# Two fused blocks on one core: where b_down's weighted sum is made, where the context's split parts are kept, and in what order the middle section stands against the context's products

## The chip, the cores and the metric

The kernel runs on one core of a Trainium2 chip. The metric is the device time of one execution in microseconds (us); the time before the change is 2914.66 us, the median of 3 runs. TensorE (PE) has two clock levels, 1.2 and 2.4 GHz; the profile gives the granted clock of a stretch as a share of the higher level, so 0.50 is 1.2 GHz.

## The reference

Two blocks run one after the other on 512 tokens of width 1024, all in float32. Cut to what the change touches:

```
# block 1: a mixer (left out), then a mixture of 32 experts, top 4
hn2 = rmsnorm(h) * (1 + sc2) + sh2
top_val, top_idx = top_k(hn2 @ router_w + router_b, 4);  gate = softmax(top_val)
for each expert e, on its own tokens x:
    g, up = split(x @ w_gu[e] + b_gu[e])
    act = (clip(up, -7, 7) + 1) * (min(g, 7) * sigmoid(1.702 * min(g, 7)))
    y[e] = act @ w_down[e] + b_down[e]
ff = sum over a token's four experts of gate * y[e]
x  = h + g2 * rmsnorm(ff)
# block 2: attention over a window, a state space model, attention over all, a gated FFN
xc  = rms_norm(ctx) * a + s                 # 256 context tokens
xn  = rms_norm(x) * a' + s'                 # 512 latent tokens (the output of block 1)
kv, dt, xbc of the context = xc @ columns of w_in
... of the latents         = xn @ columns of w_in, and so on to the output
```

b_down enters the sum as `sum_e G[token, e] * b_down[e]`, one product of the 512x32 gate matrix G with the 32x1024 matrix of biases.

## The kernel before

**Products.** TensorE multiplies in a reduced float32 form, so each operand is split into a high and a low part (`hi`, `lo`; `turnh`, `turnl`; `chh`, `chl`) and a product is made of three: hi x hi, hi x lo, lo x hi. All large weights come through one `Stream`: chunks of 128x1024 (512 KB) are loaded on the SyncE queue (SP) into `raw` tiles, ScalarE casts each to `hi` (L1573), VectorE subtracts to `lo` (L1575). Pools of three raw and three hi/lo buffers each are filled ahead of use, in the order of a list of requests; the last entry of a request says which pools it may take.

**Experts.** The router gives G. Then `go_on` runs 32 expert blocks of 128 tokens. Within them PE, ScalarE, VectorE and GpSimd (POOL) keep the order in which the code is written. Each block has three products (gate, up, down, of 8 weight chunks each), and a dictionary of hooks names what else is called behind chunk number 0 to 7 of a product: activations, transposes of the next operand, the gather of the next tokens, the scatter of the finished rows `ey` to `y_d` (L1286). Before the loop `start_sums` (L1104) transposes G to `gT`, multiplies it with `bdown` and copies the result to `k.acc`, the tile in which the four rows of each token are added later.

**Context.** `fr.b2.context()` is a generator that normalises the 256 context tokens. It is stepped once per expert from the third on, by the hook behind chunk 6 of the gate product. Each of its last steps handles one or two of 8 column groups: transposes on PE, scale and shift on VectorE (`ctmp`, L1782), the high part on ScalarE (`chp`, L1843), the low part on POOL (`clp`), and, each second group, two stores to DRAM (`chh_d`, `chl_d`) on ScalarE's queue:

```
nc.scalar.copy(part[0][:, j % 2], o)
nc.gpsimd.tensor_tensor(part[1][:, j % 2], o, f(part[0][:, j % 2]), op=OP.subtract)
if j % 2:
    for v, d in zip(part, s.ch_d):
        nc.scalar.dma_start(d[:, j - 1:j + 1], f(v))
```

**Behind the experts.** `mid` (L2767) makes block 1's result. For each of 4 tiles of 128 tokens it loads four 128x1024 tiles of rows, `my`, from `y_d` on POOL's queue (three buffers), adds each with its gate on VectorE (L2790, `scalar_tensor_tensor`), takes the norm (ScalarE squares, POOL's power `mr`, VectorE L2795 and L2796), stores x to `x_d` on ScalarE's queue, and takes the second norm (`mq`), whose factor VectorE multiplies in (L2800). `go_on` drains `mid` before `Block2.run` (L2570) starts. `run` loads `chh` and `chl` back from DRAM on SP, takes eight steps of `J.ctx` (the context's products with w_in, L1726, and L135 to L137 with the operands turned round; `put_kv` rotates and stores the keys, L1982 to L1998), then weaves the context's state space steps and the transposes of the latents (`turned_g`) with the rest of `J.ctx`, and goes on to the latents' products. From `mid` on the framework's scheduler sets each engine's order, by what is ready in the order of the code.

Of the kernel before, what the change touches and what calls it, by code (L numbers as in the profile page):

```python
# [10 lines left out]
F32 = mybir.dt.float32  # L11
# [1013 lines left out]
def router(k, A, pool, lg, counted):  # L1025
# [70 lines left out]
    k.gk = k.mk.tile([P, NT, TOPK], F32, name="gk")  # L1096
# [6 lines left out]
def start_sums(k, A, pool, G):  # L1103

    nc = k.nc
    E = NE
    bd = pool.tile([E, D], F32, name="bdown")
    nc.scalar.dma_start(bd, A["exp_b_down"][0])
    gT = pool.tile([E, T], F32, name="gT")
# [12 lines left out]
class Experts:  # L1122
# [156 lines left out]
    def out(s, b, step=None):  # L1279
        nc = s.nc  # L1280
        if step in (0, None):
            b.y = s.pool.tile([P, D], F32, name="ey", tag="ey", bufs=2)
# [76 lines left out]
def experts(fr, k, A, lg, mod1):  # L1359
# [29 lines left out]
    k.acc = k.hp.tile([P, NT, D], F32, name="acc", tag="h")  # L1389
# [38 lines left out]
    def go_on():  # L1428
# [3 lines left out]
        start_sums(k, A, rt, G)  # L1432
# [16 lines left out]
        with tc.manual_schedule(engines={E.PE, E.Activation, E.DVE, E.Pool}):  # L1449
# [3 lines left out]
            for e in range(NE):  # L1453
# [5 lines left out]

                def act(half):  # L1460
                    return lambda: x.acted(b, half)
# [3 lines left out]
                x.gate(nb, {0: act(0), 1: act(1), 3: turn(0), 4: turn(1), 6: lambda: next(side, None) if e > 1 else None})  # L1465
# [13 lines left out]
                if e + 2 == NE:  # L1479
# [6 lines left out]
                    mid = fr.b2.mid()  # L1486
                    next(mid)
# [4 lines left out]
        drain(mid)  # L1492
# [303 lines left out]
class Block2:  # L1796
# [18 lines left out]
    def context(s):  # L1815
# [11 lines left out]
        s.ch_d = [k.dp.tile([P, KJ, 256], F32, name=n) for n in ("chh_d", "chl_d")]  # L1827
# [10 lines left out]
        part = []  # L1838

        def put(j, o):  # L1840
            if j % 2 == 0:
                part[:] = [p.tile([P, 2, 256], F32R, name=n, tag=n, bufs=2) for n in ("chp", "clp")]
            nc.scalar.copy(part[0][:, j % 2], o)  # L1843
            nc.gpsimd.tensor_tensor(part[1][:, j % 2], o, f(part[0][:, j % 2]), op=OP.subtract)
            if j % 2:
# [724 lines left out]
    def run(s):  # L2570
# [23 lines left out]
        for _ in range(8):  # L2594
            next(J.ctx)
# [293 lines left out]
```

## Time and profile before

| | |
|---|---|
| median of 3 runs | 2914.66 us (2907.94 to 2918.86) |
| the profiled execution | 2916.79 us, its span 2915.0 us |
| mean granted clock | 0.962 |
| PE busy | 2697.6 us, 93% of the span |
| VectorE busy | 2197.3 us, 75% |
| ScalarE busy | 1595.3 us, 55% |
| experts, first product to last | about 420 to 1653 us from the span's start |

Times of the trace count from the start of the span. "Busy" of an engine includes matmuls that run slowly under the lower clock. In the rows of a timeline, a bracket gives how long the engine stood idle before the instruction and what released it.

### The profile page before, as it was taken

Reading aid. Unit: us, or ns where it says so; the run is one execution under the profiler, and the core shown is the slowest. Engines: PE = TensorE matmul, PEld = TensorE weight load, DVE = VectorE, ACT = ScalarE, POOL = GpSimd, SP = SyncE. Lnnn points to the kernel's source line nnn. Section 1 sums busy time; section 2 is a strip of 40 time slices with the busy share of each in tenths; the row PEclk is TensorE's granted clock in tenths of the full one; section 3 lists DMA queues with packets and bytes.
Section 4 is the critical chain, followed back from the end, with each engine's and each line's share of the span. In section 5 each row is a group of like instructions: output and inputs, shape, how many; then the busy total and the mean of one; then the engine's idle time right before and its main releaser. Section 6 shows DMA issues by size and latency. Waiting matters only on the chain. (4 is left out here: it accounts for less than half of the span.)

```text
span 2915.0 us, 37354 instructions
## 1 busy us (share of the span) xinstructions
PE 2697.6 (93%) x12897; PEld 2140.3 (73%) x12897; DVE 2197.3 (75%) x3214; ACT 1595.3 (55%) x2403; POOL 597.2 (20%) x460
## 2 busy tenths in 40 slices
PE   6789889999999999999999849998999999899998
PEld 3566638887777778888878647887688787688886
DVE  6988559999999999999999777766777555533322
ACT  3233337787777677777777543664457422443322
POOL 2654110102000010110000022001421332322222
PEclk8889889999999999999999979999999999999999
DMA  7546558999999999999999942221211565433332
GB/s 209 171 125 196 188 213 299 378 355 358 353 336 360 337 371 355 373 358 376 368 356 366 346 148 91 62 66 44 65 30 48 189 200 173 142 94 94 95 94 72
DMA packets 273119, 645.33 MB, mean 221 GB/s; under 512 B 53754, under 2 KB 99744, under 8 KB 272414
## 3 DMA queue, kind: packets, MB, share of 16 engines
q1 hardware_dynamic: 227728, 587.41, 57.5%
q10 hardware_dynamic: 33390, 30.30, 3.3%
q0 software_dynamic: 11808, 25.19, 2.4%
q8 instruction: 103, 1.69, 0.2%
q14 instruction: 90, 0.74, 0.1%
HBM read 624.33 MB, written 34.73 MB: 226 GB/s over the span
## 5 line engine op out<-in xcount | busy, mean ns | idle before, releaser
L1575 DVE TENSOR_TENSOR lo<-raw,hi 128x1024 fp32r<-128x1024 f32 x938 | 1115.5, 1232 | 303.6 <-ACT hi L1573 301.8
L1573 ACT CAST hi<-raw 128x1024 fp32r<-128x1024 f32 x997 | 1011.2, 1056 | 458.9 <-PE mm L136 132.2
L1232 PE MATMUL mm<-hi,turnh 128*128 128x512 f32 x1584 | 506.1, 401 | 0.8 <-ACT hi L1573 0.8
L1232 PE MATMUL mm<-lo,turnh 128*128 128x512 f32 x1584 | 495.2, 394 | 11.2 <-DVE lo L1575 10.8
L1232 PE MATMUL mm<-hi,turnl 128*128 128x512 f32 x1584 | 495.8, 394 | 0.0
L1232 PEld LDWEIGHTS mm<-lo,turnh 128*128 128x128 f32 x1584 | 295.9, 188 | 88.9 <-DVE lo L1575 22.7
L1232 PEld LDWEIGHTS mm<-hi,turnl 128*128 128x128 f32 x1584 | 298.4, 188 | 68.4 <-issue 1.5
L1232 PEld LDWEIGHTS mm<-hi,turnh 128*128 128x128 f32 x1584 | 287.8, 189 | 56.0 <-ACT hi L1573 2.5
L1575 POOL TENSOR_TENSOR lo<-raw,hi 128x1024 fp32r<-128x1024 f32 (+1 forms) x59 | 148.9, 2524 | 558.7 <-ACT hi L1573 524.0
L1286 POOL DMA_INDIRECT y_d<-ey,idx x33 | 50.4, 1527 | 877.7 <-ACT ey L1284 723.9
L141 ACT CAST turnh<-tr 128x512 fp32r<-128x512 f32 x132 | 77.5, 587 | 188.0 <-PE tr L221 188.0
L135 PE MATMUL mm<-lhh,hi 128*128 128x512 f32 x288 | 118.9, 413 | 0.7 <-ACT apr L2068 0.7
L1661 DVE SCALAR_TENSOR_TENSOR mvacc<-mvw,silu_c,mvacc 128x512 f32<-128x512 f32 x112 | 101.7, 908 | 22.4 <-DMA mvw<-in_w_mod_dram 17.1
L137 PE MATMUL mm<-lhh,lo 128*128 128x512 f32 x288 | 117.3, 409 | 0.0
L136 PE MATMUL mm<-lhl,hi 128*128 128x512 f32 x288 | 115.5, 401 | 0.0
L142 DVE TENSOR_TENSOR turnl<-tr,turnh 128x512 fp32r<-128x512 f32 x132 | 90.4, 685 | 4.5 <-ACT turnh L141 4.3
L2053 DVE TENSOR_REDUCE amax<-mm 128x1 f32<-128x256 f32 (+2 forms) x128 | 60.4, 501 | 41.1 <-PE mm L2048 21.1
L1726 PE MATMUL mm<-hi,lhh 128*128 128x256 f32 (+2 forms) x256 | 85.5, 338 | 3.2 <-DVE zt L2384 1.9
L2068 ACT ACTIVATE apr<-mm,negm 128x256 f32<-128x256 f32 (+2 forms) x128 | 68.6, 543 | 30.8 <-DVE negm L2058 16.4
L1726 PE MATMUL mm<-lo,lhh 128*128 128x256 f32 (+2 forms) x256 | 83.3, 326 | 1.9 <-DVE lo L1575 1.9
L1726 PE MATMUL mm<-hi,lhl 128*128 128x256 f32 (+2 forms) x256 | 82.2, 324 | 0.0
L137 PE MATMUL mm<-fhh,lo 128*128 128x512 f32 x192 | 77.2, 402 | 0.0
(752 smaller groups left out, 5168.9 us busy)
## 6 DMA issues: line engine op xcount, KB each, us to landing
raw<-in_exp_w_gu_dram SPq DMA_DIRECT2D x528, 512.0 KB
raw<-in_exp_w_down_dram SPq DMA_DIRECT2D x264, 512.0 KB
raw<-in_w_in_dram SPq DMA_DIRECT2D x83, 512.0 KB
mvw<-in_ada_w_dram SPq DMA_DIRECT2D x32, 512.0 KB
raw<-in_w_out_dram SPq DMA_DIRECT2D x32, 512.0 KB
mvw<-in_w_mod_dram SPq DMA_DIRECT2D x32, 512.0 KB
raw<-in_ffn_w_gate_dram SPq DMA_DIRECT2D x22, 512.0 KB
raw<-in_ffn_w_up_dram SPq DMA_DIRECT2D x22, 512.0 KB
```

Source lines behind the costliest of these rows:

```text
L135: k.nc.tensor.matmul(out, lh, rh, start=start, stop=False)
L136: k.nc.tensor.matmul(out, lh, rl, start=False, stop=False)
L137: k.nc.tensor.matmul(out, ll, rh, start=False, stop=stop)
L141: k.nc.scalar.copy(hi, src)
L142: k.nc.vector.tensor_tensor(lo, src, f(hi), op=OP.subtract)
L1232: nc.tensor.matmul(pss[n], a[:, j, :], c[:, n * 512:(n + 1) * 512], start=(j == 0 and i == 0), stop=(last and i == 2))
L1573: s.k.nc.scalar.copy(pm(hi[:, :m], True), pm(raw[:, :m], False))
L1575: eng.tensor_tensor(pm(lo[:, :m], True), pm(raw[:, :m], False), pm(f(hi[:, :m]), True), op=OP.subtract)
L1661: nc.vector.scalar_tensor_tensor(acc, v[:, j - q], sc(j), acc, op0=OP.mult, op1=OP.add)
L1726: k.nc.tensor.matmul(o, a[:, jj, sl], c[:, j, :], start=(jj == 0 and u == 0 and i % per == 0), stop=(jj == nk_all - 1 and u == 2), skip_gr ...
L2053: nc.vector.tensor_reduce(mx[:, i_:i_ + 1], ps[:, :n], axis=AX.X, op=OP.max)
L2068: nc.scalar.activation(b.pr[:, o:o + n // P].rearrange("p a n -> p (a n)"), ps[:, :n], AF.Exp, bias=b.nm, scale=0.125, accum_out=tile_[t]. ...
```

## The change

1. `start_sums` becomes `gates_turned`: only the transposes of G, and a store of `gT` to DRAM. The product with `bdown` is made in `mid`, per token tile, into PSUM, and the first `my` of a tile is added to it from there, in two halves.
2. The context's parts stay on chip, in a tile `chb` (in the space that `k.acc` had). Its steps are finer: transposes, then VectorE, then ScalarE, then POOL, each in a step of its own, and three hooks per expert call them (`aside`: gate 6, down 4, up 3).
3. `mid` is called in `run` and woven with `J.ctx`. All its DMAs are on POOL's queue, `my` has five buffers, its result stands in a tile `xn`, and the last factor is multiplied in by ScalarE.
4. The context's weight chunks take pool 0 alone. `ey` has one buffer, `k.gk` lies in the space of `lg`.

```diff
-def start_sums(k, A, pool, G):
+def gates_turned(k, pool, G):
...
     for t in range(NT):
-        nc.tensor.transpose(pt[:E, t * P:(t + 1) * P], G[:, t, :], k.ident)
-    nc.scalar.copy(gT, pt[:E, :])
-    for t in range(NT):
-        for n in range(2):
-            ps = tr_ps(k)
-            nc.tensor.matmul(ps, gT[:, t * P:(t + 1) * P], bd[:, n * 512:(n + 1) * 512], start=True, stop=True)
-            nc.scalar.copy(k.acc[:, t, n * 512:(n + 1) * 512], ps)
+        nc.tensor.transpose(pt[:NE, t * P:(t + 1) * P], G[:, t, :], k.ident)
+    nc.scalar.copy(gT, pt[:NE, :])
+    nc.gpsimd.dma_start(k.gT_d, gT)
...
-                x.gate(nb, {0: act(0), 1: act(1), 3: turn(0), 4: turn(1), 6: lambda: next(side, None) if e > 1 else None})
+                x.gate(nb, {0: act(0), 1: act(1), 3: turn(0), 4: turn(1), 6: aside})
...
-                hooks = {0: first, 1: lambda: x.gated(nb, 1), 2: lambda: x.gated(nb, 2), 5: step}
+                hooks = {0: first, 1: lambda: x.gated(nb, 1), 2: lambda: x.gated(nb, 2), 4: aside, 5: step}
                 x.down(b, hooks)
-                hooks = {0: lambda: x.out(b, 0), 1: lambda: x.out(b, 1), 2: step, 7: step}
+                hooks = {0: lambda: x.out(b, 0), 1: lambda: x.out(b, 1), 2: step, 3: aside, 7: step}
...
-        drain(mid)
...
+        s.chb = k.hp.tile([P, 2, KJ, 256], F32R, name="chb", tag="h")
...
-        yield from turned_g(k, tmp, xc, 2, s.a1[:, 1], s.s1[:, 1], put, 0)
+        for j in range(KJ):
+            ps = sm_ps(k)
+            for t in range(2):
+                nc.tensor.transpose(ps[:, t * P:(t + 1) * P], xc[:, t, j * P:(j + 1) * P], k.ident)
+            yield
+            o = p.tile([P, 256], F32, name="ctmp", tag="ctmp", bufs=2)
+            nc.vector.tensor_scalar(o, ps[:, :256], s.a1[:, 1, j:j + 1], s.s1[:, 1, j:j + 1], op0=OP.mult, op1=OP.add)
+            yield
+            nc.scalar.copy(s.chb[:, 0, j], o)
+            yield
+            nc.gpsimd.tensor_tensor(s.chb[:, 1, j], o, f(s.chb[:, 0, j]), op=OP.subtract)
...
-            k.st.reqs[i][5][:] = [both] * 2
+            k.st.reqs[i][5][:] = [(0,)] * 2
...
-        for v, d in zip((S.chh, S.chl), s.ch_d):
-            nc.sync.dma_start(f(v), d)
+        s.xn = chp.tile([P, NT, D], F32, name="xn")
+        middle = s.mid()
...
-        for _ in range(8):
-            next(J.ctx)
+        weave(middle, J.ctx, rate=0.6)
...
     def mid(s):
...
+        nc.gpsimd.dma_start(gT, k.gT_d)
...
-        nc.scalar.dma_start(g2b, k.g2_d.partition_broadcast(P))
+        nc.gpsimd.dma_start(bd, s.A["exp_b_down"][0])
+        nc.gpsimd.dma_start(g2b, k.g2_d.partition_broadcast(P))
...
-            nc.scalar.dma_start(hs[t], k.h_d[t * P:(t + 1) * P, :])
+            nc.gpsimd.dma_start(hs[t], k.h_d[t * P:(t + 1) * P, :])
...
-                y = p.tile([P, D], F32, name="my", tag="my", bufs=3)
+                y = p.tile([P, D], F32, name="my", tag="my", bufs=5)
                 nc.gpsimd.dma_start(y, rows[:, i])
-                nc.vector.scalar_tensor_tensor(x, y, k.gk[:, t, i:i + 1], x, op0=OP.mult, op1=OP.add)
+                if i:
+                    nc.vector.scalar_tensor_tensor(x, y, k.gk[:, t, i:i + 1], x, op0=OP.mult, op1=OP.add)
+                    continue
+                for n in range(2):
+                    c = slice(n * 512, (n + 1) * 512)
+                    ps = sm_ps(k)
+                    nc.tensor.matmul(ps, gT[:, t * P:(t + 1) * P], bd[:, c], start=True, stop=True)
+                    nc.vector.scalar_tensor_tensor(x[:, c], y[:, c], k.gk[:, t, i:i + 1], ps, op0=OP.mult, op1=OP.add)
+            yield 5.0
...
-            nc.scalar.dma_start(k.x_d[t * P:(t + 1) * P, :], h)
+            nc.gpsimd.dma_start(k.x_d[t * P:(t + 1) * P, :], h)
...
-            nc.vector.tensor_scalar(x, h, q[:, o], None, op0=OP.mult)
+            nc.scalar.mul(x, h, q[:, o])
...
+            yield 4.0
```

Three places where the order of instructions changes. The first is PE at the start of the experts, behind the products `TW,oh` that make the first slots; `mm<-hi,turnl` and its like are expert 0's gate product. Before:

```order
L1169 MATMUL sm<-TW,oh 128x4
L1232 MATMUL mm<-hi,turnl 128x512
L1117 MATMUL tr<-bdown,gT 128x512 x8
L1232 MATMUL mm<-hi,turnl 128x512
L1232 MATMUL mm<-lo,turnh 128x512 x2
L1232 MATMUL mm<-hi,turnh 128x512 x2
```

After the change, at the same place:

```order
L1162 MATMUL sm<-TW,oh 128x4
L1225 MATMUL mm<-hi,turnl 128x512 x2
L1225 MATMUL mm<-lo,turnh 128x512 x2
L1225 MATMUL mm<-hi,turnh 128x512 x2
L1225 MATMUL mm<-hi,turnl 128x512 x2
```

The eight products with `bdown` no longer stand between the two halves of the gate product's first chunk.

The second place is ScalarE within one of the experts that take a context step; `turnh` are the next operand's parts, `esg` the gate's sigmoid, `ey` the finished rows. Before, between the casts of weights:

```order
L141 CAST turnh<-tr 128x512
L1573 CAST hi<-raw 128x1024 x2
L1843 CAST chp<-ctmp 128x256
L1847 DMA chh_d<-chp 128x512
L1847 DMA chl_d<-clp 128x512
L1573 CAST hi<-raw 128x1024 x2
L1252 ACTIVATE esg<-mm 128x512 x2
```

After the change:

```order
L1245 ACTIVATE esg<-mm 128x512 x2
L1566 CAST hi<-raw 128x1024 x8
L1277 COPY ey<-mm 128x512 x2
L1566 CAST hi<-raw 128x1024 x3
L1840 CAST chb<-ctmp 128x256
L1566 CAST hi<-raw 128x1024
L141 CAST turnh<-tr 128x512
```

The cast of the context's part now stands one hook behind the VectorE instruction that writes `ctmp`, and the two stores, which wait for POOL's `clp`, are gone from ScalarE's queue.

The third place is VectorE behind the last expert; `kk` and `ks` are the context's keys, `my` the rows of block 1. Before, the context's keys stand behind all of `mid`, the end of which is:

```order
L2796 TENSOR_TENSOR mh<-mh,acc 128x1024
L149 TENSOR_SCALAR mq<-mq 128x1
L2800 TENSOR_SCALAR acc<-mh,mq 128x1024
L1982 COPY kk<-mm 128x128
L1989 TENSOR_TENSOR kk<-kk,khi 128x128
L1990 COPY ks_16013<-khi 128x2x128
```

After the change, right behind the last expert:

```order
L1568 TENSOR_TENSOR lo<-raw,hi 128x1024
L1975 COPY kk<-mm 128x128
L1568 TENSOR_TENSOR lo<-raw,hi 128x1024
L2788 SCALAR_TENSOR_TENSOR xn<-my,lg,sm 128x512 x2
L1982 TENSOR_TENSOR kk<-kk,khi 128x128
L2782 SCALAR_TENSOR_TENSOR xn<-my,lg,xn 128x1024
L1983 COPY ks_15881<-khi 128x2x128
L1984 COPY ks_15881<-kk 128x2x128
L2782 SCALAR_TENSOR_TENSOR xn<-my,lg,xn 128x1024
```

The first context keys stand among the first token tile's sums (`sm` is b_down's product, `lg` holds the gates). On POOL's queue (after the change) the loads of `gTb`, `bdown`, `g2b` and two `mh` stand ahead of the last scatter, and the later `mh` loads and the `x_d` stores between the `my` loads:

```order
L1279 DMA y_d<-ey,idx 2048x1024
L2780 DMA my<-y_d 128x1024 x7
L152 TENSOR_TENSOR mr<-mr,mhalf 128x1
L2780 DMA my<-y_d 128x1024 x2
L2796 DMA x_d<-mh 128x1024
L2780 DMA my<-y_d 128x1024
L152 TENSOR_TENSOR mq<-mq,mhalf 128x1
```

There a `my` load now stands behind a store that waits for VectorE's `mh`; before, the stores were on ScalarE's queue.

## Rows read from the trace of the kernel before

**Rows 1.** The page: busy time and slices; DMA is the engines' mean share.

```profile
PE 2697.6 (93%) x12897; PEld 2140.3 (73%) x12897; DVE 2197.3 (75%) x3214; ACT 1595.3 (55%) x2403; POOL 597.2 (20%) x460
...
PE   6789889999999999999999849998999999899998
...
PEclk8889889999999999999999979999999999999999
```

**Rows 2.** Windows: stretch, length, busy PE, PEld, DVE, ACT, POOL, PEclk, DMA, GB/s.

```profile
419.00:437.00 18.00, 17.48 (x36) 6.74 (x36) 6.32 (x13) 8.85 (x13) 1.98 (x2) 0.50 0.63 226
437.00:500.00 63.00, 63.00 (x292) 51.33 (x293) 55.94 (x60) 48.21 (x55) 3.94 (x2) 0.96 0.83 286
760.00:1050.00 290.00, 277.74 (x1269) 216.98 (x1268) 267.69 (x297) 207.72 (x248) 21.39 (x23) 1.00 0.95 349
1050.00:1600.00 550.00, 547.95 (x2563) 447.46 (x2562) 541.55 (x604) 425.64 (x488) 55.56 (x31) 1.00 0.98 365
1653.40:1720.00 66.60, 19.77 (x108) 18.80 (x108) 40.58 (x46) 15.67 (x26) 17.31 (x25) 0.63 0.81 265
1720.00:1790.00 70.00, 60.12 (x401) 53.15 (x402) 55.28 (x106) 34.18 (x68) 21.64 (x15) 0.94 0.17 56
```

**Rows 3.** Timeline of PE at the start of the experts: start, duration, instruction.

```profile
421.89 0.77 PE L1232 MATMUL mm<-hi,turnl 128*128 128x512 f32 x1
422.89 14.02 PE L1117 MATMUL tr<-bdown,gT 32*128 32x512 f32 x16 [0.23 <-ACT gT L1113]
436.84 0.80 PE L1232 MATMUL mm<-hi,turnl 128*128 128x512 f32 x1
```

**Rows 4.** Timeline of DVE in the same stretch and in the first expert.

```profile
438.75 1.23 DVE L1575 TENSOR_TENSOR lo<-raw,hi 128x1024 fp32r<-128x1024 f32 x1 [12.85 <-ACT hi L1573]
...
454.08 0.69 DVE L1257 SCALAR_TENSOR_TENSOR eg<-mm,esg 128x512 f32<-128x512 f32 x1
```

**Rows 5.** Timeline around one of the context's steps within the experts.

```profile
805.13 0.41 ACT L1843 CAST chp<-ctmp 128x256 fp32r<-128x256 f32 x1 [4.07 <-DVE ctmp L1782]
...
806.83 2.00 ACT L1573 CAST hi<-raw 128x1024 fp32r<-128x1024 f32 x2 [1.29 <-POOL clp L1844]
...
807.90 1.22 DVE L1575 TENSOR_TENSOR lo<-raw,hi 128x1024 fp32r<-128x1024 f32 x1 [2.81 <-ACT hi L1573]
```

**Rows 6.** Waits from 480 to 1640 us: total, times, longest.

```profile
ACT chp L1843 <- DVE ctmp L1782: 30.5, 8, 4.1
...
PE mm L1232 <- DVE lo L1575: 10.8, 18, 1.9
```

**Rows 7.** Timeline behind the experts, 1653 to 1721 us.

```profile
1653.75 1.06 ACT L1284 COPY ey<-mm 128x512 f32<-128x512 f32 x2
...
1662.56 0.58 PE L1726 MATMUL mm<-hi,chh 128*128 128x288 f32 x1 [9.34 <-DMA chh<-chh_d]
...
1670.20 3.95 DVE L2790 SCALAR_TENSOR_TENSOR acc<-my,gk,acc 128x1024 f32<-128x1024 f32 x3 [15.10 <-DMA my<-y_d]
...
1718.34 0.75 DVE L2800 TENSOR_SCALAR acc<-mh,mq 128x1024 f32<-128x1024 f32 x1 [0.66 <-POOL mq L152]
...
1720.34 1.08 PE L1994 MATMUL tr<-ident,ks 128*128 128x128 f32 x4 [32.48 <-DVE ks L1990]
```

**Rows 8.** VectorE's first instruction for the latents' state space steps.

```profile
1789.29 0.48 DVE L2244 MEMSET acsrw<- 64x512 f32 x1
```

**Rows 9.** The tile `my`: duration in ns min/median/max, first and last start.

```profile
L2789 POOL DMA_DIRECT2D my<-y_d x16: 527/532/582, 1664.4 to 1701.1; - x16
L2790 DVE SCALAR_TENSOR_TENSOR acc<-my,gk,acc x16: 1275/1280/1286, 1670.2 to 1709.0; 128x1024 f32<-128x1024 f32 x16
...
DMA to landing us min/median/max: 4.4/5.8/7.3
```

**Rows 10.** The tile `mh`: VectorE's multiplication by the last factor.

```profile
L2800 DVE TENSOR_SCALAR acc<-mh,mq x4: 748/753/754, 1693.5 to 1718.3; 128x1024 f32<-128x1024 f32 x4
```

**Rows 11.** DMA issues from 1620 to 1800 us: the scatters, median us to landing.

```profile
y_d<-ey,idx POOLq DMA_INDIRECT x2, 8.6
```

More of the change, by code (lines that the diff above doesn't have):

```diff
@@ L1094, in router @@
     TT(G, G, gs.unsqueeze(2).to_broadcast(sh), OP.mult)
-    k.gk = k.mk.tile([P, NT, TOPK], F32, name="gk")
+    k.gk = lg[:, :, :TOPK]
     for i in range(TOPK):
@@ L1100, in router @@
     return G
-def start_sums(k, A, pool, G):
+def gates_turned(k, pool, G):
     nc = k.nc
[L1106 to L1109, printed above, removed]
+    gT = pool.tile([NE, T], F32, name="gT")
     pt = tr_ps(k)
     for t in range(NT):
-        nc.tensor.transpose(pt[:E, t * P:(t + 1) * P], G[:, t, :], k.ident)
-    nc.scalar.copy(gT, pt[:E, :])
-    for t in range(NT):
-        for n in range(2):
-            ps = tr_ps(k)
-            nc.tensor.matmul(ps, gT[:, t * P:(t + 1) * P], bd[:, n * 512:(n + 1) * 512], start=True, stop=True)
-            nc.scalar.copy(k.acc[:, t, n * 512:(n + 1) * 512], ps)
+        nc.tensor.transpose(pt[:NE, t * P:(t + 1) * P], G[:, t, :], k.ident)
+    nc.scalar.copy(gT, pt[:NE, :])
+    nc.gpsimd.dma_start(k.gT_d, gT)
 class Experts:
@@ L1281, in out @@
         if step in (0, None):
-            b.y = s.pool.tile([P, D], F32, name="ey", tag="ey", bufs=2)
+            b.y = s.pool.tile([P, D], F32, name="ey", tag="ey", bufs=1)
             for n in range(2):
@@ L1431, in go_on @@
         nb = x.block(1)
-        start_sums(k, A, rt, G)
+        gates_turned(k, rt, G)
         es1.close()
@@ L1458, in go_on, with aside @@
                     queue.append(x.further(0, fu))
+                def aside():
+                    if e > 1:
+                        next(side, None)
                 def act(half):
@@ L1485, in go_on @@
                     fr.b2.plan()
-                    mid = fr.b2.mid()
-                    next(mid)
             x.acted(b)
@@ L1837, in context @@
             yield
[L1838 to L1845, printed above, removed]
-                for v, d in zip(part, s.ch_d):
-                    nc.scalar.dma_start(d[:, j - 1:j + 1], f(v))
-        tmp = lambda: p.tile([P, 256], F32, name="ctmp", tag="ctmp", bufs=2)
-        yield from turned_g(k, tmp, xc, 2, s.a1[:, 1], s.s1[:, 1], put, 0)
+        for j in range(KJ):
[9 more added lines that the diff above has]
+            nc.gpsimd.tensor_tensor(s.chb[:, 1, j], o, f(s.chb[:, 0, j]), op=OP.subtract)
         es.close()
@@ L2467, in jobs @@
         x = lambda: (s.hh, s.hl)
-        cx = lambda: (S.chh, S.chl)
+        cx = lambda: (s.chb[:, 0], s.chb[:, 1])
         mm = lambda: mm_ps(k)
@@ L2574, in run @@
         k.st.share = 3
+        s.wx_es.close()
         lat_es, lat = pool("lat", "left")
@@ L2578, in run @@
         ch_es, chp = pool("chp", "left")
-        S.chh = chp.tile([P, KJ, 256], F32R, name="chh")
-        S.chl = chp.tile([P, KJ, 256], F32R, name="chl")
-        for v, d in zip((S.chh, S.chl), s.ch_d):
-            nc.sync.dma_start(f(v), d)
+        s.xn = chp.tile([P, NT, D], F32, name="xn")
+        middle = s.mid()
         c_es, p = pool("ctx", "left")
@@ L2601, in run @@
         drain(J.ctx)
-        s.wx_es.close()
         ck_es, ck = pool("ctxk", "right")
@@ L2769, in mid @@
         k, nc = s.k, s.nc
-        es, p = s.pool("mid", "left")
-        ff = s.xn = k.acc
+        es, p = s.pool("mid", "right")
+        bd, gT = p.tile([NE, D], F32, name="bdown"), p.tile([NE, T], F32, name="gTb")
+        nc.gpsimd.dma_start(gT, k.gT_d)
         g2b = p.tile([P, D], F32, name="g2b")
@@ L2827, in setup @@
     k.h_d = k.dp.tile([T, D], F32, name="h_d")
+    k.gT_d = k.dp.tile([NE, T], F32, name="gT_d")
     k.y_d = k.dp.tile([TOPK * T, D], F32, name="y_d")
```

7 lines of the change are left out of this document (2 added, 5 removed).

## Prediction

> **What bounds the kernel now.** I read the page first: PE is busy for 93% of the span, at the full clock but for a few slices, and of its 40 slices two in the middle and the first ones are the thin ones [rows 1]. So time can be won where PE stands still, or where it does work that need not be on its path. I then cut the span into stretches [rows 2] at the places that the change touches, and looked in each for what ends last.
>
> Three places stand out. At the start of the experts PE is busy but runs at a granted clock of 0.50, its lower level, and inside that stretch it does 14 us of b_down's sum while the experts' first product waits behind it [rows 2, 3]. From 760 to 1050 us PE is busy for 277.74 of 290 us, from 1050 to 1600 us for 547.95 of 550: the first of the two has 12.26 us of idle time, and at the second's rate (2.05 per 550) it would have 1.08, so 11.2 us are in excess [rows 2]. The context's finer steps lie in the first and not in the second. Last, from 1653.4 to 1720 us PE works for 19.77 of 66.6 us, at 0.63 [rows 2]; it ends a wait of 32.48 us for VectorE [rows 7].
>
> **Term 1: b_down's sum leaves the start.** The eight products appear as 16 records and hold PE from 422.89 until the gate product goes on at 436.84 [rows 3]: 13.95 us. In that time VectorE stands idle for 12.85 us, since its weights ahead are all split [rows 4]. In the changed order nothing takes the products' place: the gate product's matmuls follow one another. So the experts begin 14 us sooner. Whether they stay ahead depends on the weights: PE's products, VectorE's splits and the DMA all run close to full later on (99.6%, 98.5% and 0.98 from 1050 to 1600 us [rows 2]), so that a lead once lost isn't made good. What can keep pace: VectorE has 12.85 us idle here and 63 - 55.94 = 7.1 us up to 500 us, 20 us together [rows 2, 4]; the DMA engines have (1 - 0.63) x 18 = 6.7 us and (1 - 0.83) x 63 = 10.7 us, 17.4 together [rows 2]. Both cover 14 us. I take -13.5. Bounds: -14 (all of it), and -7, if only the DMA's slack in the first stretch (6.7 us) could be used. The copies of the sums on ScalarE were no bound there (8.85 of 18 us [rows 2]) and are worth nothing.
>
> **Term 2: the context's steps in the experts.** One such step shows the mechanism [rows 5]. ScalarE, in written order, comes to the cast of `ctmp` and waits 4.07 us, because VectorE has its own queue of splits ahead of the instruction that writes it. Then the second store waits for POOL's `clp`, and the cast of the next weights starts 1.29 us late. VectorE's next split then waits 2.81 us for that cast. Over the experts ScalarE waits 30.5 us in 8 such places, up to 4.1 each, and PE 10.8 us in 18 places for a split [rows 6], which fits the 11.2 us of excess. In the changed order VectorE's instruction, ScalarE's and POOL's each come one hook later than what they wait for, some eight casts of weights apart on ScalarE, and the two stores are gone. Nothing waits for `chb` until the experts are over, so the cover is the whole rest of them. I take -8: 4.07 of the 5.36 us that ScalarE loses (76%) are the wait for `ctmp`, and 76% of 11.2 is 8.5, less a little for the hooks that are added. Bounds: -11 (all), and -4, if ScalarE still finds half of these waits. Thirty steps go over ten experts, three in each, where 14 went over 14; the early ones (squares and norms on ScalarE and POOL, as before) stay, and are in neither bound.
>
> **Term 3: behind the experts.** I measure from the last expert's `ey`, at 1653.4, to VectorE's first instruction for the latents' steps at 1789.29 [rows 2, 7, 8]: 135.9 us. Before, `mid` goes first on VectorE. It waits for its first row tile until 1670.20 (15.1 us idle) and ends at 1718.34 + 0.75 = 1719.1; the context's keys stand behind it, and PE, which has done the context's first products since 1662.56, waits for them until 1720.34 [rows 7]. Afterwards the order is mixed: keys between the sums.
>
> How short can the stretch become? VectorE's work in it is 40.58 + 55.28 = 95.9 us [rows 2]; four factors of 0.753 go to ScalarE [rows 10], and four sums of 1.28 become two halves each out of PSUM, for which the nearest row is a 128x512 of the same operation with a PSUM operand, 0.69 [rows 4, 9]: -3.0 + 4 x (1.38 - 1.28) = -2.6, so 93 us. The first row tile can't come much sooner than now: `ey` is done at about 1654.8, the scatter needs 8.6 us [rows 11], a `my` 5.8 [rows 9]; together 1669, 16 us from the start. Lower bound: 14 us until the first tile, with 3 us of keys done in it, and 90 of work without a gap, 104 us, a gain of 32. Upper bound: VectorE works at the rate that it has from 1720 to 1790 us, where it waits for PE and ScalarE (55.28 / 70 = 0.79 [rows 2]): 15 + 90/0.79 = 129, a gain of 7. Since sums and context's work now fill each other's gaps, I take a rate in the middle, 0.86: 15 + 90/0.86 = 120, a gain of 16 to 17. I take -17.
>
> What is added here beside it: eight products with `bdown`, 14.02 us of PE at the lower clock as before [rows 3]; PE has 46.8 us idle from 1653.4 to 1720 [rows 2], which is their cover; without it they would cost 7 to 14 us. Reloading `chh` and `chl` is gone, for which PE waited 9.34 us [rows 7]; what comes first now are weights that are split already. ScalarE's four products with the last factor are about 1.06 each, by its casts and copies of that size [rows 7], on an engine that is busy for 15.67 of 66.6 us [rows 2]. Fewer weight buffers for the context (pool 0 alone) matter where DMA is short; its share from 1720 on is 0.17 [rows 2]. I count these at nothing.
>
> POOL is the queue to look at: the later loads of `mh` and the stores of `x_d` join the `my` loads there, six DMAs. An issue of `my` took 0.527 to 0.582 us, with VectorE working on 1.28 us sums all the while [rows 9], so six cost 3.5 us of a queue that is busy for 17.31 of 66.6 [rows 2]. The Trainium skill speaks against the move: its page "SBUF — State Buffer", section "SBUF: two separate sides", says that descriptors of DMAs issued from GpSimd's queue are written by GpSimd itself, that VectorE in a two-port mode locks it out meanwhile, and that such a DMA then took about 3.1 us where it takes 0.62 alone. By that, six would cost an estimated 15 us more, and the sum would be 2891. The narrow spread of the sixteen issues does not agree with that, so I keep the row's figure.
>
> **Sum.** -13.5 - 8 - 17 = -38.5. Against the profiled execution, 2916.79 us (span 2915.0 and 1.8 around it), that is 2878.3; that execution lies 2.1 above the median of 2914.66, so the forecast is 2876.
>
> **Rivals.**
>
> A. *The tail fills without gaps*, beyond 32 us. For: PE's wait of 32.48 us goes whole [rows 7]. Against: the first row tile's 15 us and the VectorE's 93 us of work stay. It would give 2916.8 - 2.1 - 21.5 - 34 = 2859 or less. 0.06.
>
> B. *The tail gives nothing*: VectorE's in-order queue now has keys that wait for PE ahead of sums that are ready, and the sums that wait for DMA ahead of keys; each order of the two only shifts the wait. For: from 1720 on it waits for others a fifth of the time [rows 2]. Then only terms 1 and 2 remain: 2893. 0.12.
>
> C. *The start's gain is given back*: the weights arrive as before, and PE waits for splits in the first experts. For: DMA at 0.95 to 0.98 in the experts [rows 2]. Against: the slack worked out above. Without term 1: 2890; if half the tail goes too, 2898. 0.03.
>
> D. *Issues on POOL's queue are held up* behind VectorE, one sum of 1.28 us for each of the six: +7.7 on the chain, 2884. Against: the even 0.53 us [rows 9]. 0.03.
>
> E. *Slower.* POOL works in order; a `my` load stands behind a store of `x_d`, which waits for VectorE's `mh`, which waits for the norm. If this makes the loads go one at a time, 16 x 5.8 = 93 us [rows 9] take the place of the 48.9 us from 1670.20 to 1719.1 [rows 7]: +44, with terms 1 and 2 +22.5, so 2937. The point from which it decides: terms 1 and 2 and the gain of mixing are used up when `mid` takes 48.9 + 38.5 = 87 us, 5.5 per load. Against: in the new order seven loads stand ahead of the first norm and two or more ahead of most others, with five buffers. 0.04.
>
> That the change doesn't do what it says I exclude for parts 1 and 2, whose order is written by hand; for part 3 it is B.
>
> **How the numbers follow.** The forecast has 0.72. Its own bounds are -57 (14 + 11 + 32), 2858, and -18 (7 + 4 + 7), 2897. The range 2856 to 2896 takes in B, D and half of C and leaves out most of A, and E: about one in ten, with the forecast's own tails some two in ten. Half a per cent, 14.6 us, is about what a measurement of this kernel can tell from no change; faster than that means below 2900. Forecast, A, B and D lie below, and C mostly: 0.93; same 0.05; slower, half of E, 0.02.
>
> **What would show it.** Right: in the trace of the changed kernel PE goes from the slots' products straight through the gate product, and the experts' last product ends 18 to 25 us sooner; idle PE from 750 to 1040 us is below 5 us; ScalarE's `chb` casts start without a wait above 1 us; from `ey` to the `acsrw` memset it takes about 120 us, with no single PE wait of 20 us. Wrong: PE waits for splits in the first experts (C); the end of the experts is sooner but the stretch behind it is still 130 us or more (B), with VectorE waiting for `mm` or `my`; `my` loads 5 us apart or an issue above 1 us on POOL (D, E).

## The result, and the profile after

The changed kernel takes 2872.86 us (median of 6 runs, 2860.30 to 2876.03) against 2914.49 us for the kernel before on the same chip: ratio 0.9852, 95% interval 0.9829 to 0.9876. The forecast was 2876 us, in a range of 2856 to 2896. The sum came out; the second of its three terms did not, and stretches that stood in no term made up for most of it.

The page of the changed kernel, busy time and slices (beside [rows 1]):

```profile
PE 2696.3 (94%) x12897; PEld 2141.6 (75%) x12897; DVE 2193.3 (76%) x3214; ACT 1599.3 (56%) x2399; POOL 632.4 (22%) x472
...
PE   6789889999999999999999879999999999899998
...
PEclk8998989999999999999999979999999999999999
```

PE's work is the same. The two thin slices in the middle, 8 and 4 before, are 8 and 7 now.

To see where the time went I take marks that both programs have: the first `tr<-ident,G` on PE (the start of the experts), the start of each expert's copy `ey` on ScalarE (33 of them, the last for the additional block), the memset of `acsrw` on VectorE, and the span's end. The stretches between them, worked out from the starts in the two traces:

| stretch | before | after | difference |
|---|---|---|---|
| to the start of the experts | 419.3 | 414.0 | -5.3 |
| from there to the 1st `ey` | 66.5 | 51.5 | -15.0 |
| 1st to 9th `ey` | 290.6 | 292.4 | +1.8 |
| 9th to 16th `ey` | 273.2 | 254.4 | -18.8 |
| 16th to 32nd `ey` | 577.0 | 579.8 | +2.8 |
| last block, 32nd to 33rd `ey` | 27.2 | 32.4 | +5.2 |
| behind the experts, to `acsrw` | 135.5 | 120.5 | -15.0 |
| from there to the end | 1125.7 | 1127.9 | +2.2 |
| span | 2915.0 | 2873.0 | -42.0 |

**The start of the experts.** PE's timeline of the changed kernel, beside [rows 3]:

```profile
414.03 0.61 PE L1109 MATMUL tr<-ident,G 128*32 128x128 f32 x2 [9.01 <-SPq L1400]
...
416.62 1.20 PE L1225 MATMUL mm<-hi,turnl 128*128 128x512 f32 x2
417.62 1.05 PE L1225 MATMUL mm<-lo,turnh 128*128 128x512 f32 x2
418.48 1.05 PE L1225 MATMUL mm<-hi,turnh 128*128 128x512 f32 x2
```

The gate product runs on without the 14 us of `bdown`, and the first `ey` comes 15 us sooner behind the start.

**The experts with context steps.** The same seven experts, 9th to 16th `ey`, in windows for the split products alone (stretch, length, busy PE and PEld, PEclk, DMA share, GB/s). Before:

```profile
776.38:1049.55 273.17, 250.10 (x1010) 184.39 (x1009) 1.00 0.95 348
```

After:

```profile
757.93:1012.32 254.39, 243.85 (x1009) 186.90 (x1008) 1.00 0.98 367
```

The same thousand matmuls, at the same granted clock, were 250.10 us "busy" and are 243.85: 6.25 us of the loss stood inside busy time before, where no idle time shows them. The waits of PE's weight loads hint at what they are. Before, this line stands in the list for that window (total, times, longest); for the changed kernel's window none like it is listed:

```profile
PEld mm L1232 <- DVE lo L1575: 19.8, 26, 1.2
```

With three hooks per expert the steps also lie in earlier experts than before. From the 1st to the 16th `ey` together the gain is 17.0 us.

**Behind the experts.** The window, then the waits, of the changed kernel from the last `ey` to `acsrw` (for the first: stretch, length, busy PE, PEld, DVE, ACT, POOL, PEclk, DMA share, GB/s; for the second: total, times, longest):

```profile
1624.50:1745.10 120.60, 88.65 (x479) 72.81 (x478) 92.18 (x152) 55.43 (x99) 40.75 (x46) 0.82 0.57 181
```

```profile
PE sm L2787 <- DVE xn L2788: 10.9, 3, 7.6
DVE xn L2788 <- DMA my<-y_d: 7.3, 1, 7.3
DVE lo L1568 <- ACT hi L1566: 6.2, 2, 5.0
```

VectorE has 92.18 us of work there (the forecast had 93). The wait of 32.48 us of [rows 7] is gone. PE's longest is now at b_down's product, which waits for a PSUM tile that VectorE's sums have to free.

The stretch is VectorE's work plus its idle time, so its windows show where the 15 us lie. The first two are the kernel before, up to its first sum and from there to `acsrw`, then the same two of the changed kernel, then its `acsrw`:

```profile
1653.75:1670.20 16.45, 6.47 (x26) 6.20 (x27) 1.23 (x1) 1.07 (x3) 2.63 (x4) 0.60 1.11 351
1670.20:1789.29 119.09, 72.71 (x480) 65.04 (x480) 93.81 (x149) 47.99 (x90) 36.32 (x36) 0.81 0.39 131
1624.54:1636.41 11.87, 4.52 (x34) 4.09 (x32) 3.32 (x4) 4.57 (x8) 3.67 (x6) 0.82 0.85 254
1636.41:1745.08 108.67, 84.07 (x445) 68.66 (x446) 88.85 (x148) 50.82 (x91) 37.09 (x40) 0.82 0.54 173
...
1745.08 0.48 DVE L2237 MEMSET acsrw<- 64x512 f32 x1
```

Ahead of the first sum VectorE is idle for 8.6 us in place of 15.2, behind it for 19.8 in place of 25.3, and its work in both is 92.2 in place of 95.0. So 6.7 us of the gain lie at the first row tile, 5.5 in the gaps behind it and 2.9 in less work.

The timeline around the last `ey` shows a loss:

```profile
1614.52 1.07 POOL L2772 DMA_DIRECT2D mh<-h_d  x2
...
1617.63 0.92 ACT L1566 CAST hi<-raw 128x864 fp32r<-128x864 f32 x1 [1.20 <-DVE lo L1568]
...
1623.96 0.68 ACT L1566 CAST hi<-raw 128x576 fp32r<-128x576 f32 x1 [5.42 <-DMA raw<-in_w_in_dram]
1624.54 1.07 ACT L1277 COPY ey<-mm 128x512 f32<-128x512 f32 x2
...
1625.89 1.01 POOL L1279 DMA_INDIRECT y_d<-ey,idx  x1 [10.29 <-ACT ey L1277]
...
1631.07 2.66 POOL L2780 DMA_DIRECT2D my<-y_d  x5 [4.17 <-DMA y_d<-ey,idx]
...
1636.41 1.41 DVE L2788 SCALAR_TENSOR_TENSOR xn<-my,lg,sm 128x512 f32<-128x512 f32 x2 [7.26 <-DMA my<-y_d]
```

ScalarE waits 5.42 us for the context's third weight chunk, and the copy of the last expert's rows stands behind that cast in its queue. The loads of `g2b` and of the first two `mh` are new at this place. The kernel before issued them within the experts, some 55 us ahead of the last `ey`:

```profile
L2775 ACTq DMA_DIRECT2D g2b<-g_d x1: 327/327/327, 1598.3 to 1598.3; - x1
```

Behind it all goes faster than before: the first sum starts 11.9 us after `ey` (1636.41 - 1624.54), where it was 16.4 (1670.20 - 1653.75 [rows 7]).

POOL's queue, from the tiles `my` and `mh` (duration in ns min/median/max, first and last start):

```profile
L2780 POOL DMA_DIRECT2D my<-y_d x16: 527/544/578, 1631.1 to 1671.3; - x16
...
L2796 POOL DMA_DIRECT2D x_d<-mh x4: 536/554/576, 1650.6 to 1694.5; - x4
```

No issue is stretched by VectorE's work.

### The profile page after: what moved, and what is told of

Same layout as the page of the kernel before. It is cut to its first block, busy times and chain, and to the rows that moved or that the text cites. A ratio compares the mean times of both kernels' runs of the same rounds, so it can differ in the third digit from the quotient of the medians.

```text
span 2873.0 us, 37342 instructions
## 1 busy us (share of the span) xinstructions
PE 2696.3 (94%) x12897; PEld 2141.6 (75%) x12897; DVE 2193.3 (76%) x3214; ACT 1599.3 (56%) x2399; POOL 632.4 (22%) x472
## 4 chain that ended last, share of the span: by engine, by line
PE 69%; DVE 9%; issue 3%; ACT 2%; POOL 1%; DMA 1%; ACTq 0%; DVEq 0%; POOLq 0%; SPq 0%
PE mm L1225 35%; PE mm L1719 6%; PE mm L137 4%; PE mm L135 4%; PE mm L136 4%; DVE lo L1568 3%; PE tr L221 2%; PE sm L1719 1%; PE tr L1719 1%; PE tr L2073 1%; PE mm L1232 1%; PE sm L2100 1%; PE tr L137 1%; PE tr L136 1%; PE tr L135 1%
## 5 line engine op out<-in xcount | busy, mean ns | idle before, releaser
L1279 POOL DMA_INDIRECT y_d<-ey,idx x33 | 66.1, 2003 | 996.8 <-ACT ey L1277 756.7
```

What stands on the lines that cost most here:

```text
L1279: nc.gpsimd.indirect_dma_start(out=s.k.y_d[:, :], out_offset=bass.IndirectOffsetOnAxis(ap=b.slot[1], axis=0), in_=b.y, in_offset=None, bou ...
```

## The experiments

Times are medians, ratios those to the kernel before in the same set, with 95% intervals. Since the part ahead of the experts spreads from run to run (last section), each is read by its stretches too, measured with the marks of the table.

**1. The sum alone.** The kernel before, with b_down's sum moved:

```diff
-        start_sums(k, A, rt, G)
+        gates_turned(k, rt, G)
...
+                for n in range(2):
+                    c = slice(n * 512, (n + 1) * 512)
+                    ps = sm_ps(k)
+                    nc.tensor.matmul(ps, gT[:, t * P:(t + 1) * P], bd[:, c], start=True, stop=True)
+                    nc.vector.scalar_tensor_tensor(x[:, c], y[:, c], k.gk[:, t, i:i + 1], ps, op0=OP.mult, op1=OP.add)
```

> The kernel before, with b_down's sum alone moved behind the experts (the transposed gates go through DRAM, the sum is made in the middle section as in the changed kernel; the finished rows have one buffer, for space). Theory: the 13.95 us of the eight products leave PE's path and nothing gives them back in the experts: the first expert's finished rows come 13 to 15 us sooner, the last ones' too, and the time is 2898 to 2903. Rival (the gain is given back): PE waits for splits or loads in the first ten experts, the last expert's rows come less than 7 us sooner, and the time is above 2907.

2898.28 us, 0.993 (0.9905 to 0.9955), as expected. The first `ey` comes 50.8 us after the start (66.5 before), the 16th still 15.5 us sooner than before; the last block takes 28.5 (27.2). The stretch behind the experts is 135.5, as before: the sum costs nothing there. The theory holds and nothing is given back in the experts.

**2. The finer steps alone.** The kernel before, with the steps split and two more hooks, the stores kept:

```diff
+            yield
+            o = p.tile([P, 256], F32, name="ctmp", tag="ctmp", bufs=2)
+            nc.vector.tensor_scalar(o, ps[:, :256], s.a1[:, 1, j:j + 1], s.s1[:, 1, j:j + 1], op0=OP.mult, op1=OP.add)
+            yield
+            nc.scalar.copy(part[0][:, j % 2], o)
+            yield
+            nc.gpsimd.tensor_tensor(part[1][:, j % 2], o, f(part[0][:, j % 2]), op=OP.subtract)
+            if j % 2:
+                yield
...
-                hooks = {0: first, 1: lambda: x.gated(nb, 1), 2: lambda: x.gated(nb, 2), 5: step}
+                hooks = {0: first, 1: lambda: x.gated(nb, 1), 2: lambda: x.gated(nb, 2), 4: aside, 5: step}
```

> The kernel before, with the context's steps alone made finer and three hooks per expert; the parts still go to DRAM by ScalarE's queue and come back behind the experts. Theory (the casts of ctmp stand too close behind VectorE's instruction): ScalarE's wait for ctmp falls from 30.5 us to below 5, PE's idle time from 760 to 1050 us to below 3, and the time is 2896 to 2906. Rival (the stores on ScalarE's queue or the DMA traffic cost it): idle time stays above 8 us and the time above 2910.

2896.65 us, 0.9925 (0.9898 to 0.9952). From the 9th to the 16th `ey` it takes 253.7 us (273.2 before), which is all of what the changed kernel gains there; from the 1st to the 16th the gain is 18.9. The window of the rows that had the excess, beside [rows 2]:

```profile
760.00:1050.00 290.00, 288.67 (x1359) 235.16 (x1358) 287.77 (x313) 226.27 (x262) 48.02 (x21) 1.00 0.99 372
```

Idle time is 1.33 us, and no wait of ScalarE for `ctmp` is listed any more (30.5 us in [rows 6]). The stores on ScalarE's queue cost nothing that shows once the steps stand apart.

**3. Coarse steps in the changed kernel**, the parts on chip:

```diff
-            yield
-            o = p.tile([P, 256], F32, name="ctmp", tag="ctmp", bufs=2)
...
+        yield from turned_g(k, tmp, xc, 2, s.a1[:, 1], s.s1[:, 1], put, 0)
...
-                hooks = {0: first, 1: lambda: x.gated(nb, 1), 2: lambda: x.gated(nb, 2), 4: aside, 5: step}
+                hooks = {0: first, 1: lambda: x.gated(nb, 1), 2: lambda: x.gated(nb, 2), 5: step}
```

> The changed kernel, with the context's steps as coarse as before (transposes, VectorE, ScalarE and POOL in one step, one hook per expert), the parts still kept on chip. Theory (spacing of the steps): the waits for ctmp come back, and the time is 2881 to 2891. Rival (what helped was that nothing goes to DRAM): within 4 us of the changed kernel's 2873.

2883.91 us, 0.987 (0.984 to 0.990), 11 above the changed kernel's median. 9th to 16th `ey`: 267.8. The wait is back:

```profile
ACT chb L1832 <- DVE ctmp L1775: 29.8, 8, 4.1
```

Leaving out the stores from coarse steps is worth 273.2 - 267.8 = 5.4 us, or some 7 if the slower pace of this kernel's undisturbed experts (last section) is taken out; spacing is worth the rest of the 19, and all of it without the other.

**4. The middle section written ahead of the context's products.**

```diff
-        weave(middle, J.ctx, rate=0.6)
+        drain(middle)
+        for _ in range(8):
+            next(J.ctx)
```

> The changed kernel, with the middle section written out whole ahead of the context's products, of which eight steps follow as before; the scheduler still orders by readiness. Theory (turns in the code fill the gaps): the stretch from the last expert's rows to the latents' first VectorE instruction grows from 120.6 us by 8 to 15, and the time is 2881 to 2888. Rival (the scheduler mixes them anyway once the parts are on chip): the stretch grows by less than 4 us, and the time is 2870 to 2877.

2868.05 us, 0.9835 (0.9806 to 0.9865); the stretch is 119.3 (120.5). The theory, which is the forecast's third term as I had put it, falls: the scheduler puts context keys ahead of and between the sums on VectorE without turns in the code.

**5. The parts through DRAM, back into the same tile.**

```diff
+            if j % 2:
+                yield
+                for n, d in enumerate(s.ch_d):
+                    nc.scalar.dma_start(d[:, j - 1:j + 1], f(s.chb[:, n, j - 1:j + 1]))
...
+        for n, d in enumerate(s.ch_d):
+            nc.sync.dma_start(f(s.chb[:, n]), d)
```

> The changed kernel, with the context's parts also stored to DRAM within the experts (ScalarE's queue, a step after POOL's subtraction) and loaded back into the same tile when the experts are over, ahead of the context's products; everything else as changed. Theory (the stretch behind the experts is shorter because PE and VectorE can begin the context at once and the 2 MB are not in the scatter's way): that stretch grows from 120.6 us by 8 to 15, the last scatter takes 8 us or more to land in place of 4.9, and the time is 2880 to 2888. Rival (five buffers, early loads and POOL's queue shortened it): it grows by less than 4 us, and the time stays within 5 of 2873.

2861.20 us, 0.9828 (0.9812 to 0.9845); last block 30.0, stretch 116.1. A miss, and a wrong design: the tile was free, so the scheduler issued the reload inside the experts:

```profile
1592.14 0.44 SPq L2580 DMA_DIRECT2D chb<-chh_d  x1
1592.93 0.33 SPq L2580 DMA_DIRECT2D chb<-chl_d  x1
```

The last `ey` is at 1614.75 there. So a way through DRAM costs nothing if it is over when the experts end; whether being late costs is for run 9. Last block and stretch are 146.1 together, 6.9 less than in the changed kernel; why they are less was not looked for.

**6. The middle section's manner as before.**

```diff
-            nc.gpsimd.dma_start(hs[t], k.h_d[t * P:(t + 1) * P, :])
+            nc.scalar.dma_start(hs[t], k.h_d[t * P:(t + 1) * P, :])
...
-                y = p.tile([P, D], F32, name="my", tag="my", bufs=5)
+                y = p.tile([P, D], F32, name="my", tag="my", bufs=3)
...
-            nc.gpsimd.dma_start(k.x_d[t * P:(t + 1) * P, :], h)
+            nc.scalar.dma_start(k.x_d[t * P:(t + 1) * P, :], h)
...
-            nc.scalar.mul(x, h, q[:, o])
+            nc.vector.tensor_scalar(x, h, q[:, o], None, op0=OP.mult)
```

> The changed kernel, with the manner of the middle section as before: three buffers for the rows, the loads of h and the stores of x on ScalarE's queue, the last factor on VectorE. Theory (on chip parts alone shorten the stretch): within 4 us of the changed kernel's 120.6 in the stretch and of 2873 in time. Rival 1 (buffers and queues did it): the stretch grows by 6 us or more, 2879 or above. Rival 2 (POOL's queue costs time): it shrinks by 4 or more.

2868.11 us, 0.9849 (0.9833 to 0.9866). The stretch is 123.6, 3.0 more, and the last block 29.5, 2.9 less. These edits of part 3 together are worth nothing, by the sum of two opposite parts: of the gain in the stretch they make 3.0 us, and the last block gives them back.

**7. Pool 0 alone, in the kernel before.**

```diff
-            k.st.reqs[i][5][:] = [both] * 2
+            k.st.reqs[i][5][:] = [(0,)] * 2
```

> The kernel before, with the context's weight chunks taking pool 0 alone. Theory (fewer buffers make the casts ahead of the last expert rows wait for their load): the last block of the experts, 27.2 us before and 32.4 in the changed kernel, takes 31 to 33, and the time is 2915 to 2922. Rival (the loads on POOL's queue compete): it takes 27 to 28.5, time 2912 to 2916.

2915.75 us, 1.0019 (1.0008 to 1.0030), a time that both had allowed. The last block takes 26.8: fewer buffers don't make the cast wait. They cost 5.6 us behind the experts, 141.1 against 135.5, which I had not foreseen. ScalarE there, where no cast waits for a load and `ey` follows at once:

```profile
1647.62 0.92 ACT L1573 CAST hi<-raw 128x864 fp32r<-128x864 f32 x1 [0.46 <-PE mm L1232]
1649.00 0.67 ACT L1573 CAST hi<-raw 128x576 fp32r<-128x576 f32 x1 [0.46 <-PE mm L1232]
1649.58 1.07 ACT L1284 COPY ey<-mm 128x512 f32<-128x512 f32 x2
```

**8 and 12. The middle section's loads on SyncE's queue**, behind the context's first three chunks:

```diff
-        nc.gpsimd.dma_start(g2b, k.g2_d.partition_broadcast(P))
+        nc.sync.dma_start(g2b, k.g2_d.partition_broadcast(P))
...
-            nc.gpsimd.dma_start(hs[t], k.h_d[t * P:(t + 1) * P, :])
+            nc.sync.dma_start(hs[t], k.h_d[t * P:(t + 1) * P, :])
```

> The changed kernel, with the middle section's loads of g2b and h on SyncE's queue, where they stand behind the context's first three weight chunks. Theory of e7: the last block of the experts still takes 31 to 33 us and the time stays at 2870 to 2876. Its rival (these 1.5 MB compete with the chunks): ScalarE's wait for the third chunk falls from 5.4 us to below 2, the last block takes 28 to 29.5, and the time is 2866 to 2871.

> The changed kernel with the middle section's loads of g2b and h on SyncE's queue, once more and in more rounds, since the time to the start of the experts spreads by more than the edit's worth. If the edit is worth what the stretches of its first profile said (last block 28.3 and stretch behind the experts 116.4, together 8 us less than in the changed kernel), the two come out as 143 to 147 us together again, and the ratio to the kernel before is 0.981 to 0.985. If that profile was chance, they take 150 or more and the ratio is 0.985 to 0.987, as the changed kernel's.

2864.96 us, 0.9848 (0.9831 to 0.9864), and again 2865.40, 0.9848 (0.9830 to 0.9865). The last block takes 28.3 and 28.3, the stretch 116.4 and 117.4: together 144.7 and 145.6, where the changed kernel has 153.0. ScalarE's casts in the first of them:

```profile
1615.89 0.92 ACT L1566 CAST hi<-raw 128x864 fp32r<-128x864 f32 x1 [0.48 <-PE mm L1225]
1617.29 0.67 ACT L1566 CAST hi<-raw 128x576 fp32r<-128x576 f32 x1 [0.48 <-PE mm L1225]
1617.87 1.06 ACT L1277 COPY ey<-mm 128x512 f32<-128x512 f32 x2
```

The rival of run 7 holds: `g2b` and two `mh`, 1.5 MB that the changed kernel issues at 1613.97 to 1615.05 on another queue, kept the third chunk away. In run 12 the cast of that chunk still waits 1.79 us for its load. This version lies 6 to 8 us below the changed kernel's medians, but the intervals of the ratios overlap, so in time alone it isn't told from it.

**9. A late reload.**

```diff
-        s.chb = k.hp.tile([P, 2, KJ, 256], F32R, name="chb", tag="h")
+        s.ch_d = [k.dp.tile([P, KJ, 256], F32, name=n) for n in ("chh_d", "chl_d")]
...
-        s.xn = chp.tile([P, NT, D], F32, name="xn")
+        S.chh = chp.tile([P, KJ, 256], F32R, name="chh")
+        S.chl = chp.tile([P, KJ, 256], F32R, name="chl")
+        for v, d in zip((S.chh, S.chl), s.ch_d):
+            nc.sync.dma_start(f(v), d)
+        s.xn = k.hp.tile([P, NT, D], F32, name="xn", tag="h")
```

> The changed kernel, with the context's parts led through DRAM as before the change: small parts stored within the experts, tiles chh and chl in space that comes free only behind the experts, so that the 2 MB are loaded when the last expert's rows are leaving (the run before this one issued its reload 22 us earlier, in the experts). The middle section's result takes the tile that held the parts. Theory (parts that are there when the experts end shorten the stretch): PE waits 8 us or more for chh, the last scatter lands in 8 us or more, the context's keys stand behind the first tile's sums, and the stretch behind the experts is 128 to 136 us against 120.6 in the changed kernel and 116.0 with the early reload; time 2876 to 2888. Rival (the middle section's five buffers and early loads shortened it): below 123, time below 2876.

2874.94 us, 0.987 (0.9845 to 0.9896). The time lies just below the theory's band and in the rival's, and can't be told from the changed kernel's in the same set (0.9858, run 11). The stretch of 128.3 lies inside the theory's band, 7.8 above the changed kernel; this is one profile. The timeline around its end of the experts (last `ey` at 1617.9):

```profile
1619.62 0.52 SPq L2582 DMA_DIRECT2D chh<-chh_d  x1
1620.19 0.43 SPq L2582 DMA_DIRECT2D chl<-chl_d  x1
...
1628.82 2.62 POOL L2790 DMA_DIRECT2D my<-y_d  x5 [8.55 <-DMA y_d<-ey,idx]
1633.29 1.41 DVE L2798 SCALAR_TENSOR_TENSOR xn<-my,lg,sm 128x512 f32<-128x512 f32 x2 [14.17 <-DMA my<-y_d]
...
1634.09 2.07 PE L2797 MATMUL sm<-bdown,gTb 32*128 32x512 f32 x2 [18.32 <-DVE xn L2798]
1636.09 0.61 PE L1719 MATMUL mm<-hi,chh 128*128 128x288 f32 x1
```

The scatter's landing stands behind the 2 MB again, and the first sum starts 15.4 us after `ey` in place of 11.9. But PE doesn't wait for `chh`, as I had put it: it waits 18.32 us at the second tile's b_down product, for VectorE, with the context's products behind it in its queue. The changed kernel has the same wait, shorter (10.9 in all), and its first context products ahead of it.

VectorE's window behind the first sum:

```profile
1633.29:1746.23 112.94, 93.29 (x509) 77.54 (x510) 93.06 (x150) 53.84 (x96) 40.65 (x40) 0.80 0.56 178
```

Its idle time there is 19.9 us, as in the changed kernel (19.8), and not 25.3 as before the change. The 7.8 us are the first tile, 3.5 later, and 4.2 us of VectorE's work that the changed kernel has done by then.

**10. Runs 4 and 8 in one.**

> The changed kernel with the middle section's loads of g2b and h on SyncE's queue behind the context's first chunks (as in an earlier run, whose last block took 28.3 us and whose stretch took 116.4) and the middle section written ahead of the context's products (as in another). If the two gains of those runs are separate: last block and stretch together 141 to 145 us against 153.0 in the changed kernel, and the time is 6 to 12 us below that of the changed kernel in the same set. If turns in the code matter once the loads don't compete: together 148 or more, and the time is within 4 of it.

2869.79 us, 0.9849 (0.9828 to 0.9870); last block 27.2, stretch 121.6, together 148.8. The gains don't add: with the loads out of the way the code without turns is 3 to 4 us worse than runs 8 and 12 by its stretches, where run 4 had it 1.9 better than the changed kernel. The time can't tell it from the changed kernel.

**11. The changed kernel again.**

> The changed kernel once more, in the same set, for the two beside it. The start of the experts lay between 405 and 419 us from the span's start in ten profiles, and at 414.03 and 405.31 in two of kernels with the same code up to there; if this spread is chance, it lies elsewhere between 404 and 420 here, while the last block (32 us) and the stretch behind the experts (120 to 121 us) come out as they did.

2871.34 us, 0.9858 (0.9838 to 0.9877). Start of the experts at 414.43, last block 32.0, stretch 120.0: the two stretches as they were. The start did not move this time; it did elsewhere (below).

## Why the prediction was right, step by step

**Term 1** (forecast -13.5): -15.0 up to the first `ey`, and run 1 has it by itself. The slack of VectorE and the DMA engines that I had counted did keep pace: 15.5 us are left at the 16th `ey`. Right. Rival C (given back in the experts) falls.

**Term 2** (forecast -8, bounds -4 and -11): -18.8, and run 2 has it by itself. The mechanism was right (ScalarE's cast too close behind VectorE's instruction), and the size was off by more than half, outside the bounds. The step that failed is the first: I took PE's idle time, 11.2 us in excess, as the price. The profile counted as busy 250.10 us of products that take 243.85 without the disturbance. The kernel before told the price itself: an undisturbed expert took 35.65 us (1336.57 to 1372.22), seven in a row from the 18th `ey` on took 250.5, and the seven with context steps took 273.2. That is 22.7 in excess, of which the change took 18.8. Half of what stays is not the steps: in the changed kernel seven undisturbed experts take 252.5 (last section).

**Term 3** (forecast -17): -15.0 in the stretch, at 120.5 against a forecast of 120 (counted from 1653.4, 0.35 us ahead of the `ey` row), and +5.2 in the block ahead of it, which I had at nothing. VectorE's work was as counted, 92.2 us. The size came out by two errors that cancel. The first sum, which I had put 15 us behind `ey` and could not come before 14, started at 11.9. And VectorE's rate behind it rose from 0.79 (93.81 of 119.09 us) to 0.82 (88.85 of 108.67) only, not to 0.86: sums and keys fill less of each other's gaps than I took.

The reason that I gave was wrong beside this. Turns in the code are not it in the changed kernel (run 4; beside run 8's loads they may be worth 3 to 4 us, run 10), and buffers, queues and the last factor make 3.0 us of it, which the last block gives back (run 6). A late reload costs 7.8 of the 15 us (run 9); I had put the end of the reload at nothing. Of the other 7, 5.4 are gaps behind VectorE's first sum (25.3 us before, 19.9 in run 9). Which edit fills them isn't settled by these runs. Rivals A and B, a gain beyond 32 us and none, fall both.

Two things that stood in the sum at nothing were not free. That the loads of `h` and `g2b` cost nothing was wrong: not for POOL, as I looked at it, but for the DMA engines, where they met the chunk that ScalarE waits for ahead of the last `ey` (runs 7, 8 and 12). Pool 0 alone cost 5.6 us behind the experts in the kernel before (run 7); what it costs in the changed kernel no run shows. A third is open, that PE's idle time covers b_down's products: PE waits for VectorE at them with the context's products behind, 10.9 us in the changed kernel, 18.3 in run 9. Whether these waits cost time isn't shown; in run 1 the same products left the stretch at 135.5.

**POOL's queue.** The issues took 0.527 to 0.578 us with VectorE at work, also those of `x_d`; rival D falls. The price worked out from the Trainium skill's page "SBUF — State Buffer" (section "SBUF: two separate sides") doesn't show either, but this trace hardly tests it: the page's 3.1 us were taken beside a VectorE `tensor_copy`, and the issues here stood beside two-input operations of VectorE or none, three of them also beside a copy or scaling of 0.29 us at most. Of the sixteen issues that the prediction held against the page, one stood beside a multiplication by a factor and took 0.572 us, the others beside two-input operations or none. The row tiles were issued five at once, then in ones and twos, all within 40 us (1631.1 to 1671.3) in place of E's 93: rival E falls too.

**The sum** was right by compensation, and so by luck as to its closeness: term 2 gave 11 us more than forecast and term 1 1.5 more; the last block took back 5, the experts 4.6 (+1.8 and +2.8), the end 2.2, and term 3 is 2 short. The 5.3 us ahead of the experts stood in no term; whether they are chance isn't settled (last section). Of the signs that I had named, one missed: the experts' last product ended 34.5 us sooner (1653.22 before, 1618.75 now), not 18 to 25, mostly by term 2's size and these 5.3 us.

## What to carry to other kernels

Where a loop repeats, price a disturbance by the spacing of a mark in it, against the loop's own undisturbed spacing, and not by an engine's idle time: that showed half of it. An instruction that needs another engine's result belongs a whole piece of queued work behind it; the distance between the steps was worth 19 us, and once they stood apart, keeping the stores off DRAM gave nothing more in the experts that these runs show. And before a load is moved as free, look at which transfers are in flight when it is issued, and who waits for them in order; 1.5 MB on another queue delayed the last expert by 4 us.

## What was not expected of the hardware

The time from the span's start to the start of the experts spreads: 405.3, 406.8, 409.8, 412.5, 413.9 to 414.4 (five times), 416.0 and 418.9 us in the profiles of kernels with the changed start of the experts, 415.5, 419.0 and 419.3 with the old one. One kernel run twice had 414.0 and 414.4 (the changed one), another 412.5 and 418.9 (runs 8 and 12). The spread among kernels with the same code up to there is up to 14 us, more than the 8 us that run 8 is worth, which may be why medians of a few runs could not tell those versions apart. The granted clock of this stretch is 0.91 and 0.92 in the two shortest and 0.89 to 0.90 in the six longest of all fourteen; what sets it was not looked for. The three with the old start lie at 415.5 and above, nine of the eleven with the new one at 414.4 and below, so a part of the 5.3 us may be the change's own.

The scatter of the last rows landed in 4.9 us in the changed kernel, 8.6 before (the median of two, [rows 11]), 9.3 in run 9 with 2 MB of loads issued behind it on another queue, 7.5 in run 8 and 6.5 in run 12.

From the 16th to the 32nd `ey` all ten profiles of kernels built from the changed one took 579.7 to 579.9 us, the four of those built from the one before 576.2 to 577.8; PE is busy for 99% of it and more in both. An undisturbed expert takes 36.01 us in the first ten and 35.65 to 35.67 in the others, with the same 164 matmuls; what makes the difference stays open.
